# Gated recurrences in chunks of 64 in place of 128, with state products split by head over two PSUM banks

## The chip, the cores and the metric

The kernel runs on one core of one Trainium2 chip. The metric is the time of one execution on the device in microseconds (us). The kernel before took 2409.89 us, the median of three runs (2408.58 to 2411.97). All the traces named here are of single profiled executions on that core. PE is the matrix engine (PEld its weight loads), DVE the vector engine, ACT the scalar engine, POOL the general engine, SP the engine that issues most transfers. PSUM is the memory that PE writes its results to; it has eight banks, and a bank holds 128 partitions x 512 fp32 values.

## The reference, cut to what matters

One layer of a decoder trunk on 2048 tokens of width 1024. A token mixer holds three kinds of heads side by side: four retention heads, eight HGRN2 heads and four GLA heads. The last two are gated linear recurrences with a decay per key channel, which the change is mostly about. A convolution-gated MLP follows.

```python
def gated_state_chunkwise(q, k, v, log_f):
    # S_t = diag(exp(log_f_t)) S_{t-1} + k_t^T v_t,  o_t = q_t S_t, in chunks of 64
    def step(s, inp):
        qn, kn, vn, gn = inp
        cum = jnp.cumsum(gn, axis=2)
        rel = jnp.where(causal, cum[:, :, :, None, :] - cum[:, :, None, :, :], -jnp.inf)
        attn = jnp.einsum('bhid,bhjd,bhijd->bhij', qn, kn, jnp.exp(rel))
        o = jnp.einsum('bhij,bhje->bhie', attn, vn) + jnp.einsum('bhid,bhde->bhie', qn * jnp.exp(cum), s)
        last = cum[:, :, -1:, :]
        s_new = jnp.exp(last[:, :, 0, :])[..., None] * s + jnp.einsum('bhjd,bhje->bhde', kn * jnp.exp(last - cum), vn)
        return s_new, o
```

Every head has 64 value columns and a key width of 64 (32 for GLA). The result does not depend on the chunk length that a kernel picks.

## The kernel before, in words

**Blocks and units.** The 2048 tokens are cut into four blocks of 512 (`NB`, `TB`), and each block into four pieces of 128 (`NCH`). Heads come in units that fill the 128 partitions: four `h` units of two HGRN2 heads each, one `g` unit of four GLA heads (two halves, called subs), and two `r` units of two retention heads. In a block they run in the order h0, g, h1, h2, h3, r0, r1. Tiles carry the unit's name: `uh2_1` is the tile u of unit h1 in block 2. Every fp32 product here is made either from three fp32r products (`split3`, lines 292 to 294: the large projections, called gemms below) or as a plain fp32 product, which shows as two records in the trace.

**A gated unit** (`gated`, L713). The scores inside a piece of 128 tokens are built level by level: at level s (1, 2, 4 ... 64) the second half of every stretch of 2s tokens attends to the first half (`level`, L753), after q and k have been multiplied by the decays of that level (`faded`, L730, on DVE). `laid` (L771) puts the level's scores into the tile `at`. The levels are issued two at a time; level 64 stands alone. Then k is transposed (`kT`, L834), the state products are made (`u`, L843: per piece, keys of 128 tokens against values of 128 tokens), `carry` (L679) runs the recurrence over the four pieces on DVE, one `scalar_tensor_tensor` of 128x64 per piece, and copies the states into a block-diagonal tile W with ACT. `attn_out` (L664) makes the output of each piece: q against W (K = 128 rows, N = 128 columns) and per head the scores against the values (K = 128, N = 64), both as four products of 32 output rows that lie in four column groups of PE's array (`tiled`, L148). ACT copies the output out of PSUM, `post` normalises it, and 21 us later by the planner's clock `transposed` (L652) turns it round for the output projection.

**PSUM.** Four banks belong to the gemms (`acc_ps`), two to the levels (`lev_ps`) and two to everything that comes late in a unit (`late_ps`, L155): the diagonal products `dt` of the first level, kT, u, the output o, the transposed output oT, and the sums of squares `ss` and broadcasts `bc` of a norm (`rstd`, L363). A tile of `late_ps` can only be written when the readers of the tile that had its bank are done.

**What sets the order.** The program is written out once, and a small planner with its own clock (`Clock`) decides where between the gemms the steps of a unit are put: each step advances the clock by a constant (`adv(MO)` and the like) and asks to be called again after a gap (`yield`). Steps with a pair of times (`RIDE`) may ride along at a `clock.pick()` of another unit, or go alone at the later time. PE, DVE and ACT each work strictly through their own list; so a PE instruction that waits holds up all gemms behind it.

Of the kernel before, what the change touches and what calls it, by code (L numbers as in the profile page):

```python
# [49 lines left out]
M512, M256, MF, ML, MT, MO, MS = 0.227, 0.12, 0.224, 0.5, 0.44, 1.7, 0.85  # L50
# [74 lines left out]
def trunk(ctx, tc, xT, vecs, cvec, cst, rope, msk, wada, win, walow, wgla, wout, wup, wdown, out):  # L125
# [486 lines left out]
    wide = [p1.tile([P, NCH, P], F32, tag=f"W{i}", name=f"W{i}") for i in range(3)]  # L612
    for st in wide:
        G.memset(st[:], 0.0)
# [49 lines left out]
    def attn_out(name, b, attn, v, qn, W):  # L664


        ps = late_ps("o" + name)
        for c in range(NCH):
            oc = ps[:, c * P:(c + 1) * P]
            inter = not (b == 0 and c == 0)  # L670
            if inter:
                tiled(oc, qn[:, c * P:(c + 1) * P], W[:, c, :], stop=False)
            for hh in range(2):
                at, col = attn[hh]
                tiled(oc[:, hh * 64:hh * 64 + 64], at[:, (c * 2 + col) * P:(c * 2 + col + 1) * P],
                      v[:, c, hh * 64:hh * 64 + 64], start=not inter, stop=hh == 1 or not inter)
        return ps

    def carry(b, Sst, ps, decay):  # L679

        W = wide.pop(0)
        wide.append(W)
        at = pu.tile([P, NCH - 1, 64], F32, tag="Sc", name="Sc", bufs=2)
        halves = slice(0, 64), slice(64, P)
        if b:
            for rs in halves:
                S.copy(W[rs, 0, rs], Sst[rs, :])
        for c in range(NCH):
            last = c == NCH - 1
            dst, u = Sst[:] if last else at[:, c, :], ps[:, c * 64:c * 64 + 64]  # L690
            if b == 0 and c == 0:
                V.tensor_copy(dst, u)
            elif not last or b < NB - 1:
                V.scalar_tensor_tensor(dst, at[:, c - 1, :] if c else Sst[:], decay(c), u, op0=ALU.mult, op1=ALU.add)
        for rs in halves:
            S.copy(W[rs, 1:NCH, rs], at[rs, :, :])
        return W

    LEVELS = [1, 2, 4, 8, 16, 32, 64]
    EOFF = {2: 0, 4: 256, 8: 384, 16: 448, 32: 480, 64: 496, 128: 504}  # L700
# [12 lines left out]
    def gated(name, b, ui, pos, kq, q, decay, subs, qk, sel):  # L713
# [16 lines left out]
        def faded(li):  # L730

            s, ev = LEVELS[li], tree[li]
            nn = TB // (2 * s)
            qv = q[:].rearrange("p h (n t s) -> p h n t s", t=2, s=s)[:, :, :, 1, :]
            kv = kq[:].rearrange("p (n t s) -> p n t s", t=2, s=s)[:, :, 0, :]

            def of_q():
                return V.tensor_tensor(qv, qv, ev[:, :, 0:1].unsqueeze(1).to_broadcast([P, 2, nn, s]), op=ALU.mult)

            def of_k():  # L740
                return V.tensor_tensor(kv, kv, ev[:, :, 1:2].to_broadcast([P, nn, s]), op=ALU.mult)
            for op in (of_q, of_k) if li < 6 else (of_k, of_q):
                done_ = op()
            marked(done_)
# [8 lines left out]
        def level(li, first):  # L753

            s = LEVELS[li]
            w = max(32, 2 * s)
            o = 0 if first else 128
            for c in range(NCH):
                for k0 in [g for g in range(0, P, 32) if g % w < max(s, 32)]:
                    r0 = k0 // w * w  # L760
                    at = c * P + r0
                    n, p0 = (c, k0) if s <= 16 else (c // 2, k0 + s * (c % 2))
                    for ps, rs in zip(pss, parts):
                        if first:
                            rhs = qc[rs, :, at // 2:(at + w) // 2].rearrange("p h (n s) -> p h n s", s=s)
                        else:
                            rhs = q[rs, :, at:at + w].rearrange("p h (n t s) -> p h n t s", t=2, s=s)[:, :, :, 1, :]
                        T.matmul(ps[p0:p0 + 32, o + n * w:o + (n + 1) * w].rearrange("p (h n s) -> p h n s", h=2, s=s),
                                 (kc_ if first else kq)[rs, c * P + k0:c * P + k0 + 32], rhs, start=True, stop=True)

        def laid(li, first):  # L771
# [3 lines left out]
            o = 0 if first else 128  # L775
            cols = slice(o, o + (128 if s < 64 else 256))
# [21 lines left out]
        for li in range(0, 8, 2):  # L798
            pss = [lev_ps(f"lv{name}_{li}") for _ in parts]
            pair_ = li < 6  # L800
# [4 lines left out]
            if pair_:  # L805
                level(li, True)
                level(li + 1, False)
            else:
                level(li, False)
            with tc.high_priority(offset=CHAIN):  # L810
                faded(li + 1 if pair_ else li)
                if li < 4:
                    ahead(li + 2)
                if li == 0:
                    pairs = dots[:, 0:NCH * nh].rearrange("p (a n) -> p a n", n=len(subs))
                    for i, near in enumerate(nears):
                        V.copy_predicated(near[:], m_all[:, 80:112].unsqueeze(1).to_broadcast([P, 8, 32]),
                                          pairs[:, :, i:i + 1].to_broadcast([P, 8, 32]))
                laid(li, pair_)
                if pair_:  # L820
                    laid(li + 1, False)
                if li < 4:
                    faded(li + 2)
            adv((2 if pair_ else 1) * ML)
# [4 lines left out]
            if pair_:  # L829
                yield PAIR_GAP[two]  # L830
        yield 4.0
# [4 lines left out]
        with tc.high_priority(offset=CHAIN):  # L836
            S.copy(kT[:].rearrange("p c n -> p (c n)"), ps[:])
            if not two:
                r0, r1 = subs[0][0][1]
                S.copy(q[r0:r1, 0, :], q[r0:r1, 1, :])  # L840
# [11 lines left out]
        for i, (rows, v, sg) in enumerate(subs):  # L852
            if i:
                yield RIDE[1]
            o = pu.tile([P, NCH, P], F32, tag="o", name=f"o{name}_{i}")
            heads = [(at, i) for at in attns] if two else [(attns[0], hh) for hh in range(2)]
            ps = attn_out(f"{name}_{i}", b, heads, v, q[:, i, :], W)
            adv(MO)
            with tc.high_priority(offset=CHAIN):
                S.copy(o[:].rearrange("p c e -> p (c e)"), ps[:])  # L860
# [127 lines left out]
    def retention(nm, b, r, pos, a, kk, kc, q, vsg):  # L988
# [16 lines left out]
        with tc.high_priority(offset=CHAIN):  # L1005
            W = carry(b, Sst, ps, lambda c: gc)
# [17 lines left out]
        ps = attn_out(nm, b, [(at, hh) for hh in range(2)], v, qn, W)  # L1024
        o = pu.tile([P, NCH, P], F32, tag="o", name="o" + nm)
        qd = c_all[:, C_QD + 2 * r:C_QD + 2 * r + 2]
        with tc.high_priority(offset=CHAIN):
            V.tensor_tensor(o[:].rearrange("p c (h e) -> p c h e", e=64),
                            ps[:].rearrange("p (c h e) -> p c h e", h=2, e=64),
                            qd.unsqueeze(1).unsqueeze(3).to_broadcast([P, NCH, 2, 64]), op=ALU.mult)  # L1030
# [786 lines left out]
```

## Time and profile before

| | us |
|---|---|
| median of three runs | 2409.89 |
| profiled execution, first to last instruction | 2407.7 |
| PE busy | 2364.9 (98%) |
| DVE busy | 1818.2 (76%) |
| ACT busy | 1292.1 (54%) |
| level products of the h units made from q itself (N = 32, 64 and 128: levels up to 16, level 32, level 64) | 15.7, 7.2, 10.3 |
| output products against W: h, g, r | 26.1, 12.5, 12.3 |
| output products against v: h, g, r | 27.4, 13.4, 13.8 |
| state products u: h, r, g | 10.5, 5.2, 2.6 |

The profiled execution lies 2.2 us below the median of the runs, so its parts can be read as parts of that median. The token mixer and what is interleaved with it take about the first 1100 us; the MLP follows. Busy time of a group is the union of its own records, so that groups that alternate, as the last but one and the last but two rows do, are counted twice for part of the time. A matmul record of some 200 to 400 ns overlaps its neighbours: how much a batch costs is read from the starts, not from the durations.

### The profile page before, as it was taken

The numbers are of one execution on the slowest core, as the hardware profiler recorded it, in microseconds if no ns is written. First come the engines' busy times: TensorE is split into PE (matmuls) and PEld (weight loads), VectorE is DVE, ScalarE is ACT, GpSimd is POOL, SyncE is SP. The second block draws the span as 40 slices with busy tenths as digits, with TensorE's granted clock in tenths as the row PEclk, the third lists the DMA queues.
The fourth block names the chain that finished last, engine by engine and source line by source line (L and its number), as shares of the span: only waits on it lengthen the run. The fifth ranks groups of instructions, "written<-read, shape, count | busy, mean of one in ns | idle before, by whom it ended". The sixth has DMA issues, their size and how long they took to land.

```text
span 2407.7 us, 51890 instructions
## 1 busy us (share of the span) xinstructions
PE 2364.9 (98%) x20523; PEld 1961.5 (81%) x20523; DVE 1818.2 (76%) x3391; ACT 1292.1 (54%) x2311; POOL 153.9 (6%) x275
## 2 busy tenths in 40 slices
PE   7999999999999999999999999999999999999998
PEld 5787878888788888887888888888878888888887
DVE  7687866868577746877988888866888787778566
ACT  4675456744665457644555454554555555455452
POOL 1000100000000100001000000000010100000000
PEclk9999999999999999999999999999999999999999
DMA  7655676797788867788554444687765444548663
GB/s 272 234 187 185 235 262 236 279 330 261 255 305 296 279 203 276 266 280 280 171 172 154 143 158 145 225 282 223 240 198 166 145 149 145 150 151 277 205 198 116
DMA packets 228884, 525.78 MB, mean 218 GB/s; under 512 B 25848, under 2 KB 28832, under 8 KB 228640
## 3 DMA queue, kind: packets, MB, share of 16 engines
q1 hardware_dynamic: 225440, 511.98, 63.7%
q0 software_dynamic: 3200, 10.49, 1.2%
q8 instruction: 161, 2.64, 0.4%
q14 instruction: 83, 0.68, 0.1%
HBM read 392.87 MB, written 129.50 MB: 217 GB/s over the span
## 4 chain that ended last, share of the span: by engine, by line
PE 82%; DVE 8%; DMA 5%; ACT 4%; issue 1%; SPq 0%; DVEq 0%; POOL 0%; ACTq 0%
PE X L292 6%; PE X L294 6%; PE X L293 6%; PE dX L292 4%; PE dX L293 4%; PE dX L294 4%; PE Z L293 3%; PE Z L294 3%; PE Z L292 3%; PE psqkvgr L292 3%; PE psqkvgr L294 2%; PE psqkvgr L293 2%; PE y L292 2%; PE y L293 2%; PE y L294 2%; PE dY L292 2%
## 5 line engine op out<-in xcount | busy, mean ns | idle before, releaser
L293 PE MATMUL X<-B,A 128*128 128x512 f32 x572 | 222.8, 389 | 0.3 <-DVE B L1187 0.3
L292 PE MATMUL X<-B,A 128*128 128x512 f32 x572 | 223.0, 390 | 0.0
L294 PE MATMUL X<-B,A 128*128 128x512 f32 x572 | 222.6, 389 | 0.0
L1187 DVE TENSOR_TENSOR dA<-rd,dA 128x512 fp32r<-128x512 f32 x154 | 106.2, 690 | 91.3 <-ACT dA L1186 91.0
L1186 ACT CAST dA<-rd 128x512 fp32r<-128x512 f32 x154 | 95.6, 622 | 145.7 <-PE dX L294 62.8
L292 PE MATMUL dX<-dB,dA 128*128 128x512 f32 x396 | 154.0, 389 | 0.0
L293 PE MATMUL dX<-dB,dA 128*128 128x512 f32 x396 | 154.0, 389 | 0.0
L294 PE MATMUL dX<-dB,dA 128*128 128x512 f32 x396 | 154.0, 389 | 0.0
L1187 DVE TENSOR_TENSOR A<-s,A 128x512 fp32r<-128x512 f32 x176 | 120.6, 686 | 37.8 <-ACT A L1186 37.7
L1186 ACT CAST A<-s 128x512 fp32r<-128x512 f32 x176 | 108.6, 617 | 60.7 <-PE Z L294 43.5
L292 PE MATMUL psvgh<-hvgh,ha 128*128 128x256 f32 x480 | 139.6, 291 | 0.0
L293 PE MATMUL psvgh<-lvgh,ha 128*128 128x256 f32 x480 | 135.7, 283 | 0.0
L294 PE MATMUL psvgh<-hvgh,ha 128*128 128x256 f32 x480 | 135.6, 283 | 0.0
L293 PEld LDWEIGHTS X<-B,A 128*128 128x128 f32 x572 | 107.4, 188 | 23.2 <-DVE B L1187 1.1
L292 PEld LDWEIGHTS X<-B,A 128*128 128x128 f32 x572 | 107.4, 188 | 22.9 <-ACT u L1493 0.7
L294 PEld LDWEIGHTS X<-B,A 128*128 128x128 f32 x572 | 107.4, 188 | 22.1
L293 PE MATMUL Z<-B,A 128*128 128x512 f32 x308 | 120.6, 392 | 2.3 <-DVE B L1187 2.1
L292 PE MATMUL Z<-B,A 128*128 128x512 f32 x308 | 120.3, 391 | 0.2
L294 PE MATMUL Z<-B,A 128*128 128x512 f32 x308 | 119.9, 389 | 0.0
L1186 ACT CAST A<-r 128x512 fp32r<-128x512 f32 x132 | 82.3, 624 | 63.8 <-PE Z L294 58.2
L1187 DVE TENSOR_TENSOR A<-r,A 128x512 fp32r<-128x512 f32 x132 | 90.6, 687 | 31.3 <-ACT A L1186 30.7
L1187 DVE TENSOR_TENSOR dB<-rb,dB 128x512 fp32r<-128x512 f32 x154 | 105.6, 687 | 7.5 <-ACT dB L1186 7.1
(491 smaller groups left out, 6786.4 us busy)
## 6 DMA issues: line engine op xcount, KB each, us to landing
gs<-yv SPq DMA_DIRECT2D x154, 256.0 KB, 3.0
rb<-gs SPq DMA_DIRECT2D x154, 256.0 KB, 4.3
r<-wup SPq DMA_DIRECT2D x143, 256.0 KB, 3.4
s<-sumsu SPq DMA_DIRECT2D x132, 256.0 KB, 3.2
wada<-wada SPq DMA_DIRECT2D x48, 512.0 KB, 4.5
rd<-sumsd SPq DMA_DIRECT2D x88, 256.0 KB, 4.2
rd<-wdown SPq DMA_DIRECT2D x66, 256.0 KB, 3.9
x<-xT SPq DMA_DIRECT2D x64, 256.0 KB, 5.3
```

The source lines that it names most:

```text
L292: T.matmul(ps, lhs[0], rhs[0], start=first, stop=False, skip_group_check=more)
L293: T.matmul(ps, lhs[0], rhs[1], start=False, stop=False, skip_group_check=more)
L294: T.matmul(ps, lhs[1], rhs[0], start=False, stop=last, skip_group_check=more)
L1186: S.copy(hi, src)
L1187: marked(V.tensor_tensor(lo, src, hi, op=ALU.subtract))
```

## The change

Gated units now work in chunks of 64: level 64 is gone, `carry` makes eight states a block, and u is made per chunk of 64 tokens, that is with 64 rows, the even chunks from partitions 0 to 63 into one late bank and the odd ones from partitions 64 to 127 into another. The products of q with the states are made per head, 64 rows and 64 columns each, head 0 into one late bank and head 1 into another, for gated and for retention units (these keep chunks of 128). The block-diagonal tiles W, their zeroing and the ACT copies into them are gone, as is a copy of half of q; the states are used from the tile Sc in which DVE leaves them. The output is copied out of PSUM by two ACT instructions of 128x256; for retention units these take the scaling that one DVE instruction did. The planner's cost of an output step, `MO`, goes from 1.7 to 1.3, and a `yield 4.0` and one `clock.pick()` vanish with level 64.

```diff
-M512, M256, MF, ML, MT, MO, MS = 0.227, 0.12, 0.224, 0.5, 0.44, 1.7, 0.85
+M512, M256, MF, ML, MT, MO, MS = 0.227, 0.12, 0.224, 0.5, 0.44, 1.3, 0.85
...
-    def attn_out(name, b, attn, v, qn, W):
-        ps = late_ps("o" + name)
+    def attn_out(name, b, attn, v, ql, Sc, chunk):
+        pss = [late_ps(f"o{name}_{hh}") for hh in range(2)]
         for c in range(NCH):
-            oc = ps[:, c * P:(c + 1) * P]
-            inter = not (b == 0 and c == 0)
-            if inter:
-                tiled(oc, qn[:, c * P:(c + 1) * P], W[:, c, :], stop=False)
-            for hh in range(2):
+            cs = slice(c * 64, c * 64 + 64)
+            carried = [g for g in range(0, P, 32) if b or chunk(c, g)]
+            for hh, ps in enumerate(pss):
+                for g in carried:
+                    T.matmul(ps[g:g + 32, cs], ql(hh)[:, c * P + g:c * P + g + 32],
+                             Sc[hh * 64:hh * 64 + 64, chunk(c, g), :], start=True, stop=False)
+            for hh, ps in enumerate(pss):
                 at, col = attn[hh]
-                tiled(oc[:, hh * 64:hh * 64 + 64], at[:, (c * 2 + col) * P:(c * 2 + col + 1) * P],
-                      v[:, c, hh * 64:hh * 64 + 64], start=not inter, stop=hh == 1 or not inter)
-        return ps
+                for g in range(0, P, 32):
+                    k0 = (c * 2 + col) * P + g
+                    T.matmul(ps[g:g + 32, cs], at[:, k0:k0 + 32], v[:, c, hh * 64:hh * 64 + 64],
+                             start=g not in carried, stop=True)
+        return pss
...
-    LEVELS = [1, 2, 4, 8, 16, 32, 64]
+    LEVELS = [1, 2, 4, 8, 16, 32]
...
-        ps = late_ps("u" + name)
+        pss = [late_ps(f"u{name}_{n}") for n in range(2)]
         for c in range(NCH):
-            tiled(ps[:, c * 64:c * 64 + 64], kT[:, c, :],
-                  lambda g: subs[g // 32 % len(subs)][1][:, c, g // 64 * 64:g // 64 * 64 + 64])
+            for n, ps in enumerate(pss):
+                rs = slice(64 * n, 64 * n + 64)
+                for g in range(0, P, 32):
+                    T.matmul(ps[g:g + 32, c * 64:c * 64 + 64], kT[rs, c, g:g + 32],
+                             subs[g // 32 % len(subs)][1][rs, c, g // 64 * 64:g // 64 * 64 + 64], start=True, stop=True)
         with tc.high_priority(offset=CHAIN):
-            W = carry(b, Sst, ps, lambda c: cur[:, c:c + 1])
+            Sc = carry(b, Sst, [pss[n % 2][:, n // 2 * 64:n // 2 * 64 + 64] for n in range(8)], lambda n: cur[:, n:n + 1])
...
             with tc.high_priority(offset=CHAIN):
-                S.copy(o[:].rearrange("p c e -> p (c e)"), ps[:])
+                for hh, ps in enumerate(pss):
+                    S.copy(o[:, :, hh * 64:hh * 64 + 64], ps[:, 0:256].rearrange("p (c e) -> p c e", e=64))
```

Three places show what the change does to the lists of the engines. In the rows, 32x64 is the shape of one product's output, "x4" four such products one after another.

PE, the output of unit h1 in block 2. Before, both kinds of products take 128 rows of the array (q against W1, then the scores ath against the values vh):

```order
L151 MATMUL oh2_1_0_10428<-W1_115,qbh2_1_9410 32x128 x4
L151 MATMUL oh2_1_0_10428<-vh2_1_9423,ath2_1_0_9475 32x64 x8
L151 MATMUL oh2_1_0_10428<-W1_115,qbh2_1_9410 32x128 x4
L151 MATMUL oh2_1_0_10428<-vh2_1_9423,ath2_1_0_9475 32x64 x8
L151 MATMUL oh2_1_0_10428<-W1_115,qbh2_1_9410 32x128 x4
```

Now the L670 rows take 64 rows of the array and the L676 rows 128:

```order
L670 MATMUL oh2_1_0_0_10662<-Sc_10490,qbh2_1_9634 32x64 x4
L670 MATMUL oh2_1_0_1_10663<-Sc_10490,qbh2_1_9634 32x64 x4
L676 MATMUL oh2_1_0_0_10662<-vh2_1_9646,ath2_1_0_9761 32x64 x4
L676 MATMUL oh2_1_0_1_10663<-vh2_1_9646,ath2_1_0_9761 32x64 x4
L670 MATMUL oh2_1_0_0_10662<-Sc_10490,qbh2_1_9634 32x64 x4
L670 MATMUL oh2_1_0_1_10663<-Sc_10490,qbh2_1_9634 32x64 x4
```

The 32-row products alternate between the two forms four times in an output, and the output fills two late banks where it filled one. Over the whole program PE's list goes between 64-row and 128-row products of 32 columns 246 times where it did so 7 times.

PE, where unit h2 of block 2 begins. Before, its diagonal products dth2_2 stood between the transposes and the state products of unit h1:

```order
L768 MATMUL lvh2_1_6_9993<-qbh2_1_9410,kh2_1_9171 32x128 x8
...
L834 MATMUL kTh2_1_10123<-c_all_86,kh2_1_9171 128x128 x4
...
L151 MATMUL dth2_2_10138<-c_all_86,qkh2_2_9910 32x2 x16
...
L768 MATMUL lvh2_2_2_10255<-qc_112,kc_113 32x32 x16
...
L151 MATMUL uh2_1_10296<-vh2_1_9423,kTh2_1_10128 32x64 x16
```

Now they stand right behind the state products, and wait for DVE:

```order
L819 MATMUL kTh2_1_10294<-c_all_86,kh2_1_9470 128x128 x4
...
L830 MATMUL uh2_1_0_10456<-vh2_1_9646,kTh2_1_10299 32x64 x4
L830 MATMUL uh2_1_1_10457<-vh2_1_9646,kTh2_1_10299 32x64 x4
...
L151 MATMUL dth2_2_10501<-c_all_86,qkh2_2_10220 32x2 [waits DVE_49,PE_49]
L151 MATMUL dth2_2_10501<-c_all_86,qkh2_2_10220 32x2 x15
```

The level-64 products (lvh2_1_6) are gone. What dth2_2 waits for is the seventh of the eight DVE steps of `carry` that read uh2_1_0, whose bank it takes.

DVE, the carry of unit h3 in block 2. Before, four steps, each but the last with one other instruction behind it:

```order
L694 SCALAR_TENSOR_TENSOR Sc_11243<-S3_108,eh2_3_10212,uh2_3_11226 128x64 [waits PE_49]
L983 TENSOR_TENSOR kkr2_0_10758<-ra1r2_0_11151,c_all_86 128x512 [waits DVE_49]
L694 SCALAR_TENSOR_TENSOR Sc_11243<-Sc_11243,eh2_3_10212,uh2_3_11226 128x64 [waits DVE_49]
L1068 TENSOR_TENSOR wsu15_0_11203<-wsu15_0_11203,wsu15_1_11204 128x512
...
L694 SCALAR_TENSOR_TENSOR S3_108<-Sc_11243,eh2_3_10212,uh2_3_11226 128x64 [waits DVE_49]
```

Now eight, with seven others between them:

```order
L691 SCALAR_TENSOR_TENSOR Sc_11601<-S3_108,eh2_3_10569,uh2_3_0_11567 128x64 [waits PE_49]
L965 TENSOR_TENSOR rb1r2_0_11509<-ra1r2_0_11507,roper2_0_11134 128x8x32
L691 SCALAR_TENSOR_TENSOR Sc_11601<-Sc_11601,eh2_3_10569,uh2_3_1_11568 128x64 [waits DVE_49,PE_49]
L966 TENSOR_TENSOR ra1r2_0_11507<-ra1r2_0_11507,roper2_0_11134 128x512 [waits DVE_49]
...
L1052 TENSOR_TENSOR wsu15_2_11561<-wsu15_1_11560 128x512 [waits DMAHW7_49,DMAHW4_49]
L691 SCALAR_TENSOR_TENSOR Sc_11601<-Sc_11601,eh2_3_10569,uh2_3_0_11567 128x64 [waits DVE_49]
L1053 TENSOR_TENSOR wsu15_2_11561<-wsu15_2_11561,wsu15_0_11559 128x512 [waits DMAHW6_49,DVE_49]
L691 SCALAR_TENSOR_TENSOR S3_108<-Sc_11601,eh2_3_10569,uh2_3_1_11568 128x64 [waits DVE_49]
```

On PE the transposes oTh2_2 now come three gemm products behind uh2_3 (twelve before), and wait for the seventh of these steps.

More of the change, by code (lines that the diff above doesn't have):

```diff
@@ L692, in carry @@
+        return pss
+    def carry(b, Sst, us, decay):
+        Sc = pu.tile([P, 8, 64], F32, tag="Sc", name="Sc", bufs=2)
+        if b:
+            S.copy(Sc[:, 0, :], Sst[:])
+        for n, u in enumerate(us):
+            last = n == len(us) - 1
+            dst = Sst[:] if last else Sc[:, n + 1, :]
+            if b == 0 and n == 0:
                 V.tensor_copy(dst, u)
             elif not last or b < NB - 1:
-                V.scalar_tensor_tensor(dst, at[:, c - 1, :] if c else Sst[:], decay(c), u, op0=ALU.mult, op1=ALU.add)
@@ L828, in gated @@
                 yield None
[L829 to L831 removed]
+            yield PAIR_GAP[two]
         ps = late_ps("kT" + name)
```

72 lines of the change are left out of this document (24 added, 48 removed).

## The prediction

> **What bounds the kernel now.** First the page: its span, PE's busy time, PE's row and the clock's row of the 40 slices, and the chain of waits by engine.
>
> ```profile
> span 2407.7 us, 51890 instructions
> PE 2364.9 (98%) x20523; PEld 1961.5 (81%) x20523; DVE 1818.2 (76%) x3391; ACT 1292.1 (54%) x2311; POOL 153.9 (6%) x275
> PE   7999999999999999999999999999999999999998
> PEclk9999999999999999999999999999999999999999
> PE 82%; DVE 8%; DMA 5%; ACT 4%; issue 1%; SPq 0%; DVEq 0%; POOL 0%; ACTq 0%
> ```
>
> PE is never at rest after the first slices, and the chain that ended last runs on it for 82% of the span. What the change does to PE's list, and every wait that it puts there, therefore shows in the time; DVE (76% busy) and ACT (54%) matter by when they let PE go on. The busy times by stretch (columns: span, then PE, PEld, DVE, ACT, POOL busy, clock, DMA) say how little PE waits in the mixer:
>
> ```profile
> 100.00:600.00 500.00, 489.19 (x6937) 411.96 (x6936) 382.90 (x938) 289.37 (x592) 26.18 (x46) 1.00 0.70 243
> 600.00:1100.00 500.00, 495.36 (x6942) 413.51 (x6941) 345.00 (x883) 289.68 (x601) 25.25 (x45) 1.00 0.78 273
> ```
>
> Idle are 10.8 + 4.6 = 15.4 us. The MLP after 1100 us is not touched.
>
> **Level 64 goes.** PE's timeline where it stood alone (start, length, then what):
>
> ```profile
> 218.87 0.40 PE L294 MATMUL psqkvgr<-hqkvgr,ha 128*128 128x512 f32 x1
> 219.19 0.64 PE L768 MATMUL lvh<-qbh,kh 128*32 128x128 f32 x16
> 219.77 0.50 PE L292 MATMUL psqkvgr<-hqkvgr,ha 128*128 128x512 f32 x1
> 220.10 0.40 PE L293 MATMUL psqkvgr<-lqkvgr,ha 128*128 128x512 f32 x1
> 220.34 0.39 PE L294 MATMUL psqkvgr<-hqkvgr,ha 128*128 128x512 f32 x1
> ```
>
> From 218.87 to 220.10 are 1.23 us, where two gemm steps take 0.46: the batch costs 0.77. Of 20 units 16 have it alone; 4 share the entry with another batch and save the products' own 0.46 only. 16 x 0.77 + 4 x 0.46 = 14.2 us gained. The removed batches would take 16 entries from gemm to 32-column products out of PE's list, and it has only 11 fewer (127 before, 116 now), so 5 x (0.77 - 0.46) = 1.5 us come back.
>
> **The outputs pay for changing the array's form.** The end of an output, and the retention scores (64 rows) behind it:
>
> ```profile
> 1056.05 0.43 PE L151 MATMUL oh<-W,qbh 128*32 128x128 f32 x8
> ...
> 1056.95 0.40 PE L151 MATMUL oh<-W,qbh 128*32 128x128 f32 x8
> 1057.17 0.41 PE L151 MATMUL oh<-vh,ath 128*32 128x64 f32 x16
> 1057.40 0.40 PE L151 MATMUL oh<-W,qbh 128*32 128x128 f32 x8
> 1057.61 0.41 PE L151 MATMUL oh<-vh,ath 128*32 128x64 f32 x16
> 1057.95 1.16 PE L1015 MATMUL scr<-qr,kcr 64*32 64x128 f32 x64
> ```
>
> A piece takes 0.45 us, 0.22 for W and 0.23 for the scores. Between batches of one form the next begins 0.18 before the last has ended (1057.17 + 0.41 against 1057.40); at the step from 128*32 to 64*32 it is 0.07 (1057.61 + 0.41 against 1057.95), so 0.11 is lost, and the first batch of a form is 0.03 longer (0.43 against 0.40). The way back, from 64 to 128 rows, is there too:
>
> ```profile
> 114.16 0.51 PE L768 MATMUL lvg<-qbg,kg 64*32 64x64 f32 x30
> 114.60 0.43 PE L151 MATMUL oh<-vh,ath 128*32 128x64 f32 x16
> ...
> 372.92 0.72 PE L768 MATMUL lvg<-qc,kc 64*32 64x32 f32 x62
> ```
>
> Again 0.07 of overlap and 0.43 for the first. I take 0.14 a change. The 64-row records come one per 8.7 ns (0.72 less one record's 0.19, over 61) to 10 ns (0.51 less 0.23, over 29), so the 16 new products against the states take 0.15 where W took 0.22. An output: 4 x (0.15 - 0.22) + 7 changes x 0.14 = +0.70; 32 outputs, +22.4 us. Bounds: 0.11 a change gives +0.49 (15.7), and 0.17 gives +0.91 (29). The Trainium skill's page TensorEngine Tiling (Array Packing) says under Key Properties that a change of the tiling mode, not of the tile alone, drains the engine. By that rule the edit loses, and these rows agree. Under Theoretical Speedup the same page has up to 2x for a small dimension of at most 64. By that alone the outputs would get cheaper, as in the third rival below, which gives 2388.
>
> **State products.** 32 records become 64 of 64 rows:
>
> ```profile
> 776.59 0.65 PE L151 MATMUL uh<-vh,kTh 128*32 128x64 f32 x32
> ...
> 780.03 0.60 PE L656 MATMUL oTh<-c_all,oh 128*128 128x128 f32 x4
> ```
>
> 0.65 less one record's 0.22 is 0.43; 64 x 9 ns are 0.58: +0.15 x 20 units = +3.0 us. PE's own work thus grows by 22.4 + 3.0 + 1.5 - 14.2 = +12.7 us (bounds +4 and +19).
>
> **The larger part: PE waits for late banks.** The state products now hold both late banks, and the next user of a bank waits on PE, with all gemms queued behind it, until the seventh of the eight carry steps has read it. DVE's timeline for the unit just shown:
>
> ```profile
> 780.47 0.28 DVE L694 SCALAR_TENSOR_TENSOR Sc<-S,eh,uh 128x64 f32<-128x64 f32 x1
> 780.66 0.69 DVE L983 TENSOR_TENSOR kkr<-ra1r,c_all 128x512 f32<-128x512 f32 x1
> 781.26 0.28 DVE L694 SCALAR_TENSOR_TENSOR Sc<-Sc,eh,uh 128x64 f32<-128x64 f32 x1
> 781.45 0.69 DVE L1068 TENSOR_TENSOR wsu<-wsu,wsu 128x512 f32<-128x512 f32 x1
> 782.06 0.28 DVE L694 SCALAR_TENSOR_TENSOR Sc<-Sc,eh,uh 128x64 f32<-128x64 f32 x1
> ```
>
> With another instruction between them the steps come 0.80 apart; the first began 3.2 us after the products' end (777.24). The transposes at 780.03 took the other bank, before the steps were done: that way out is gone. With next to nothing between, steps come 0.31 apart:
>
> ```profile
> 747.96 0.27 DVE L694 SCALAR_TENSOR_TENSOR Sc<-Sc,eh,uh 128x64 f32<-128x64 f32 x1
> 748.15 0.16 DVE L182 TENSOR_SCALAR rsn<-msn 128x4 int32<-128x4 int32 x1
> 748.27 0.28 DVE L694 SCALAR_TENSOR_TENSOR Sc<-Sc,eh,uh 128x64 f32<-128x64 f32 x1
> ```
>
> Other instructions in the way, and what frees the banks of dots and outputs:
>
> ```profile
> L738 DVE TENSOR_TENSOR qbh<-qbh,eh 128x512 f32<-128x512 f32 x96 | 66.5, 692 | 5.1 <-ACT qc L749 2.6 <-PE lvh L768 2.1
> L741 DVE TENSOR_TENSOR kh<-kh,eh 128x256 f32<-128x256 f32 x96 | 40.3, 420 | 4.7 <-PE lvh L768 4.7
> L817 DVE COPY_PREDICATED nearh<-m_all,dth x16: 439/445/461, 72.5 to 1012.3; 128x256 f32<-128x256 uint32 x16
> L860 ACT COPY oh<-oh 128x512 f32<-128x512 f32 x16 | 9.3, 583 | 4.8 <-PE oh L151 4.6
> ```
>
> The waits, by the new lists:
>
> - Transposes three gemm products (0.7 us, and 0.1 for the entry) behind u of h3, four times. Three have an instruction between every two steps: 6 x 0.80 + 0.28 = 5.1; block 0 has four such: 4 x 0.80 + 2 x 0.31 + 0.28 = 4.1. Less 0.8, with the first step 1 us late (0 at the best, 3.2 in the rows above): 3 x 5.3 + 4.3 = 20.2.
> - Transposes behind u of h2, blocks 1 to 3. One step, three others (0.4, 0.69, 0.42), six steps: 3.6; the first held back some 0.9 by the level work in front of it; less 0.8: 3.7 x 3 = 11.1.
> - Diagonal products of h2 directly behind u of h1, blocks 1 to 3: 0.28 + 0.69 + 6 x 0.31, with 0.1 to start: 2.9 x 3 = 8.7.
> - Four more users 1.4 to 2 us behind u: about 1 each, 4.
> - 17 places where a bank's user comes within 2 us of the last one, waiting for one copy of a dot (0.45), an output (0.58 at most) or a transpose: 0.65 each, 11.
>
> Sum 55.0; with no step late and 0.2 at the small places 38; with the first step 3.2 late at h3, and DVE and ACT as far behind elsewhere, 87. Other engines catch up while PE waits, so I let a third of the 15.4 us of present idle time go: -4 (bounds 0 and -15). On DVE itself the lost decays of level 64 (0.692 + 0.420) and the four added steps (4 x 0.28) cancel; ACT only loses work. Both stay off the path except in these waits.
>
> **The sum.** 2407.7 + 12.7 + 55.0 - 4 = 2471.4 in the span of the profiled execution; the runs' median lies 2.2 above it: **2474 us**. The bounds add up to 2407.7 + 4 + 38 - 15 + 2.2 = 2437 and 2407.7 + 19 + 87 + 2.2 = 2516.
>
> **Rivals.** *The clock falls* (2495): waits of 4 to 5 us are as long as this one at the start:
>
> ```profile
> 8.60:13.20 4.60, 0.01 (x1) 0.00 (x0) 3.37 (x5) 4.29 (x8) 0.00 (x0) 0.90 1.02 388
> 13.20:19.00 5.80, 5.65 (x18) 4.10 (x19) 4.70 (x17) 2.72 (x4) 0.00 (x0) 0.50 1.03 416
> ```
>
> After 4.6 us of rest the granted clock was 0.50 for 5.8 us, half of which is lost, 2.9; at the seven longest waits that is 20 us. Against it: the other long waits lie below 4. The Trainium skill (TensorE: Matmul & The Clock Gate, Part 1: The HAM clock gate) puts the fall after an idle window of about 3.4 us; these two rows agree.
>
> *The banks are free in time* (2423): if DVE runs ahead and the small places cost nothing, only PE's 12.7 us stay. For it: DVE has a quarter of its time free. Against: a chain of dependent steps cannot be shorter than 7 x 0.31 = 2.2.
>
> *Row packing pays and nothing waits* (2388): 64-row products side by side without loss at a change save 32 x 4 x 0.07 = 9 in the outputs beside the 14.2, less 3.0 and 1.5, and some idle goes: -21. It decides only if a change costs under 0.04 us. The rows say 0.11.
>
> *The parts cancel* (2410): changes at 0.11, half the gain of level 64 more from shared entries, waits within the present idle.
>
> **Chances.** Forecast 0.64, clock 0.14, free banks 0.12, cancel 0.04, packing 0.06. The two below and half of the free-bank case lie outside the range at the low end, some of the clock's case at the high end: 2428 to 2506; the forecast's own range is 2437 to 2498. What the measurement can tell from no change is 0.2% (4.8 us): faster 0.06, within 0.04, slower 0.90.
>
> **What would show it.** In the waits of PE, rows of oTh and dth released by the carry, some 40 us together; PE idle in 100 to 1100 of 50 to 80 us; outputs about 0.7 us longer between the first and last start; clock row still 9. Wrong is it if PE's idle time stays near 15 us, or an output is no longer than before.

## The result and the profile after

The changed kernel took 2517.05 us, the median of four runs (2512.88 to 2520.79), against 2409.69 us for the kernel before on the same chip: a ratio of 1.0441, 95% interval 1.0426 to 1.0456. It is slower, as forecast, but by 107 us where 64 were forecast, and outside the range. The profiled execution took 2515.09 us and its span is 2513.0 us, 105.3 more than the span before.

The page after, in the rows that were read before: span, busy times, PE's and the clock's row of the 40 slices, and the chain of waits by engine.

```profile
span 2513.0 us, 54320 instructions
PE 2413.6 (96%) x21787; PEld 1983.0 (79%) x21787; DVE 1816.9 (72%) x3403; ACT 1252.3 (50%) x2210; POOL 153.0 (6%) x272
PE   7998999889998999989999999999999999999998
PEclk9999999999998999999999999999999999999999
PE 80%; DVE 9%; DMA 5%; ACT 4%; issue 2%; SPq 0%; DVEq 0%; POOL 0%; ACTq 0%
```

PE is busy 48.7 us longer and idle 56.6 longer. The clock's row shows one 8 among the nines, and it would be easy to pass over. The busy times by stretch (span, PE, PEld, DVE, ACT, POOL, then the clock) say more:

```profile
100.00:600.00 500.00, 462.43 (x6926) 379.84 (x6925) 346.73 (x867) 248.53 (x506) 22.21 (x41) 0.96 0.63 219
600.00:1100.00 500.00, 473.15 (x6824) 389.46 (x6823) 319.05 (x808) 255.91 (x499) 23.68 (x40) 0.97 0.70 243
```

In the 1000 us where PE rested 15.4 us before it now rests 64.4, and the mean clock is 0.96 and 0.97 where it was 1.00. What PE waits for (total, times, longest):

```profile
PE oTh L653 <- DVE Sc L691: 25.9, 7, 5.3
PE dth L151 <- DVE Sc L691: 13.8, 4, 5.3
...
PE ssn L151 <- DVE Sc L691: 4.2, 2, 3.6
```

These 43.9 us are waits for the carry to leave a late bank. The kernel before has one such wait, of 2.0 us:

```profile
PE ssn L151 <- DVE S L694: 2.0, 1, 2.0
```

One of the new ones on PE's timeline, block 0 (start, length, then what):

```profile
240.43 0.86 PE L830 MATMUL uh<-vh,kTh 64*32 64x64 f32 x64
...
241.80 0.40 PE L294 MATMUL psqkvgr<-hqkvgr,ha 128*128 128x512 f32 x1
246.38 1.09 PE L653 MATMUL oTh<-c_all,oh 128*128 128x128 f32 x4 [4.19 <-DVE Sc L691]
...
249.40 0.63 PE L294 MATMUL psqkvgr<-hqkvgr,ha 128*128 128x512 f32 x1
249.83 0.63 PE L292 MATMUL psqkvgr<-hqkvgr,ha 128*128 128x512 f32 x1
...
251.58 0.39 PE L294 MATMUL psqkvgr<-hqkvgr,ha 128*128 128x512 f32 x1
251.81 0.40 PE L292 MATMUL psqkvgr<-hqkvgr,ha 128*128 128x512 f32 x1
```

The wait is 4.19 us. What the forecast had left to a rival stands behind it: gemm products that begin 0.23 us apart at 251.6 begin 0.43 apart at 249.4. The same place in stretches of 3.4 us:

```profile
240.90:244.30 3.40, 1.29 (x35) 0.71 (x29) 3.40 (x10) 0.00 (x0) 0.00 (x0) 1.00 0.19 76
244.30:247.70 3.40, 1.32 (x6) 1.25 (x7) 2.15 (x7) 0.19 (x1) 0.00 (x0) 0.50 0.69 233
247.70:251.10 3.40, 3.40 (x9) 2.64 (x8) 0.75 (x1) 0.50 (x1) 0.00 (x0) 0.50 0.00 0
251.10:254.50 3.40, 3.40 (x16) 2.81 (x15) 1.22 (x1) 1.05 (x1) 0.00 (x0) 1.00 0.02 5
```

The granted clock is 0.50 for 6.8 us, and runs on at half speed after PE is busy again. Between 100 and 1150 us the trace has 18 such periods, 6 of 6.8 us and 12 of 3.4: 82 us. The kernel before has none between 43 us and its end.

So the 105 us have three parts. I take each PE record from its start to the next start (or its own end), price those that lie in a half-clock period at the mean of their kind at full clock, and call what is left of them "clock". Against the kernel before, in us:

| profiled run | ratio of the runs (95%) | span | PE's own work | PE idle | clock |
|---|---|---|---|---|---|
| changed kernel | 1.0441 (1.0426, 1.0456) | +105.3 | +13.2 | +56.6 | +35.5 |
| e1_evac | 1.0192 (1.0177, 1.0207) | +50.5 | +14.1 | +17.4 | +18.9 |
| e2_grouped | 1.0366 (1.0345, 1.0386) | +92.9 | -6.0 | +64.9 | +34.0 |
| e3_both | 1.0125 (1.0099, 1.0151) | +27.5 | -4.2 | +23.1 | +8.7 |
| e6_busy | 1.0462 (1.0445, 1.0480) | +111.2 | +76.2 | +24.7 | +10.3 |
| e6b_busy6 | 1.0371 (1.0346, 1.0397) | +91.0 | +47.9 | +33.0 | +10.0 |
| e7_outputs | 1.0141 (1.0120, 1.0161) | +43.4 | +21.1 | +15.5 | +6.8 |
| e10_dots | 1.0116 (1.0100, 1.0131) | +28.9 | -1.2 | +22.6 | +7.5 |
| e11_dots_kt | 1.0129 (1.0114, 1.0144) | +34.5 | -3.7 | +25.7 | +12.3 |
| e12_onebank | 1.0076 (1.0061, 1.0091) | +18.5 | -6.7 | +15.6 | +9.6 |
| e13_rest1 | 1.0149 (1.0132, 1.0166) | +38.9 | +6.5 | +24.7 | +7.6 |
| e14_rest2 | 1.0302 (1.0284, 1.0320) | +70.9 | -1.1 | +45.1 | +26.7 |
| e15_mo | 1.0398 (1.0370, 1.0426) | +101.7 | +12.1 | +51.3 | +38.1 |

The division between own work and clock is good to some 8 us: e13_rest1 and e14_rest2 carry the same added products and differ by 7.6 us in own work. With medians in place of means the parts of the changed kernel come out the same, and when kinds are drawn otherwise its clock's part lies between 30 and 36 us and its own work between 13 and 19. Each ratio is to runs of the kernel before beside it.

### The profile page after: what moved, and what is told of

It reads as the page before. It is cut to its first block, busy times and chain, and to the rows that moved or that the text cites. A ratio compares the mean times of both kernels' runs of the same rounds, so it can differ in the third digit from the quotient of the medians.

```text
span 2513.0 us, 54320 instructions
## 1 busy us (share of the span) xinstructions
PE 2413.6 (96%) x21787; PEld 1983.0 (79%) x21787; DVE 1816.9 (72%) x3403; ACT 1252.3 (50%) x2210; POOL 153.0 (6%) x272
## 4 chain that ended last, share of the span: by engine, by line
PE 80%; DVE 9%; DMA 5%; ACT 4%; issue 2%; SPq 0%; DVEq 0%; POOL 0%; ACTq 0%
PE X L292 6%; PE X L294 6%; PE X L293 6%; PE dX L293 4%; PE dX L294 4%; PE dX L292 4%; PE Z L293 3%; PE Z L294 3%; PE Z L292 3%; PE psqkvgr L292 2%; PE psqkvgr L293 2%; PE psqkvgr L294 2%; PE y L292 2%; PE y L294 2%; PE y L293 2%
## 5 line engine op out<-in xcount | busy, mean ns | idle before, releaser
L1175 DVE TENSOR_TENSOR A<-s,A 128x512 fp32r<-128x512 f32 x176 | 120.5, 686 | 38.4 <-ACT A L1174 38.2
L293 PEld LDWEIGHTS X<-B,A 128*128 128x128 f32 x572 | 107.3, 188 | 23.1 <-DVE B L1175 0.9
```

The costliest lines, as they stand in the source:

```text
L293: T.matmul(ps, lhs[0], rhs[1], start=False, stop=False, skip_group_check=more)
L1175: marked(V.tensor_tensor(lo, src, hi, op=ALU.subtract))
```

## The experiments

**Free the banks at once** (e1_evac)**.** In the changed kernel, two ACT copies take the state products out and the carry reads the copy:

```diff
+        us = pu.tile([P, 2, 256], F32, tag="us", name="us" + name, bufs=1)
         with tc.high_priority(offset=CHAIN):
-            Sc = carry(b, Sst, [pss[n % 2][:, n // 2 * 64:n // 2 * 64 + 64] for n in range(8)], lambda n: cur[:, n:n + 1])
+            for n, ps in enumerate(pss):
+                S.copy(us[:, n, :], ps[:, 0:256])
+            Sc = carry(b, Sst, [us[:, n % 2, n // 2 * 64:n // 2 * 64 + 64] for n in range(8)], lambda n: cur[:, n:n + 1])
```

> The changed kernel, with one thing added in the gated units: two ACT copies take both banks of the state products (128x256 each) into SBUF at once, and the carry steps read them there, so the banks are free after the copies and not after the seventh carry step. PE's list is the same. Theory W (waits for the two banks, and the halved clock that follows each such wait, are most of the 105 us): PE waits behind the carry, 43.9 us now in the rows of oTh, dth and ssn, fall below 10; PE idle from 100 to 1150 us goes from 72 to about 35; the half-clock periods from 18 to about 7 (those of other causes); time about 2455 us, 2440 to 2470. Theory P (PE's own longer work, outputs above all, is most of it, and the waits only move): 2495 to 2515. Theory D (DVE is late whatever it reads; the outputs would then wait for the states in place of the banks): the idle time stays above 60 us in other rows, over 2490.

2458.8 us (2455.4 to 2460.2), ratio 1.0192. In the traces PE's list is the same but for four places, where the records of two small batches stand in another order. In its waits the carry is gone, and the copies stand in its place:

```profile
PE oh L670 <- DVE msn L373: 4.0, 2, 3.1
...
PE dth L151 <- ACT ush L835: 3.4, 3, 1.8
...
PE oTh L653 <- ACT ush L835: 2.1, 3, 0.7
```

The group of the copies (after the bar: busy time and mean ns of one):

```profile
L835 ACT COPY ush<-uh 128x256 f32<-128x256 f32 x32 | 10.4, 381 | 5.2 <-PE uh L830 4.7
```

43.9 us of waits became 5.5, idle time from 100 to 1150 us went from 72 to 32, and the clock's part from 35.5 to 18.9. Half-clock periods fell from 18 to 10, three more than expected. Theory W holds; P and D fall.

**One change of form in an output** (e2_grouped)**.** The same products, those against the states first:

```diff
+        def put(hh, g, c, lhs, rhs, stop):
+            T.matmul(pss[hh][g:g + 32, c * 64:c * 64 + 64], lhs, rhs, start=(hh, g) not in begun, stop=stop,
+                     skip_group_check=True)
+            begun.add((hh, g))
         for c in range(NCH):
...
+            for hh in range(2):
+                for g in [g for g in range(0, P, 32) if b or chunk(c, g)]:
+                    put(hh, g, c, ql(hh)[:, c * P + g:c * P + g + 32], Sc[hh * 64:hh * 64 + 64, chunk(c, g), :], False)
+        for c in range(NCH):
...
+                    put(hh, g, c, at[:, k0:k0 + 32], v[:, c, hh * 64:hh * 64 + 64], c == NCH - 1)
```

> The changed kernel, with the same products of each output in another order: first all products against the states (64 rows) of the four pieces, then all score products (128 rows), so one change of the array's form in the output and not seven. Nothing else moves on PE. Theory F (a change of form costs 0.10 to 0.14 us each, which is why an output takes 2.53 us and 1.90 before): an output takes 1.75 to 1.95 us, and the time falls by 32 x 6 x 0.13 = 25 us to about 2492, 2487 to 2500. Theory R (the longer output is the two heads' separate products, twice as many 64-row records, and changes of form are nearly free): an output stays within 0.2 us of 2.53 and the time within 2512 to 2521.

2500.99 us (2494.7 to 2503.8), ratio 1.0366. PE's timeline of one output, first of the changed kernel (its first and last batches and the gemm behind it), then of this one:

```profile
1081.24 0.34 PE L670 MATMUL oh<-Sc,qbh 64*32 64x64 f32 x16
1081.51 0.43 PE L676 MATMUL oh<-vh,ath 128*32 128x64 f32 x16
...
1083.41 0.43 PE L676 MATMUL oh<-vh,ath 128*32 128x64 f32 x16
1083.77 0.50 PE L292 MATMUL pshqh<-ha,hhqh 128*128 128x512 f32 x1
```

```profile
1072.14 0.86 PE L668 MATMUL oh<-Sc,qbh 64*32 64x64 f32 x64
1072.93 1.10 PE L668 MATMUL oh<-vh,ath 128*32 128x64 f32 x64
1073.96 0.50 PE L292 MATMUL pshqh<-ha,hhqh 128*128 128x512 f32 x1
```

From start to the next gemm 2.53 us against 1.82: 0.71 for six changes, 0.12 each. That is theory F, though the time stands 1 us above its range: it fell by 0.75% (18 us) and not by 32 x 0.71 = 23, for PE's own work fell 19 us and its idle time grew 8. PE came sooner to the same late banks.

**Both** (e3_both)**.**

> Both edits together: state products copied out at once, and one change of form in each output. If the two act on different things the gains add: 2517 less about 62 (the copies) less about 25 (the order) is 2430, 2412 to 2446. If the shorter outputs only bring PE sooner to the same late banks, the second gain is lost: 2450 or more. Below the kernel before (2409.7) only if the other small waits go as well.

2440.43 us (2437.0 to 2450.7), ratio 1.0125. The two gains add, within the range given: with the banks free, the shorter outputs keep their worth.

**Useless work in place of rest** (e6_busy, e6b_busy6)**.** Behind u at the ten places of the carry's longest waits:

```diff
+        if ui == 3 or b and ui in (1, 2):
+            keep_going(lev_ps("idle" + name), 13)
```

> The changed kernel, with useless work added: 13 matmuls (128x256, some 2.7 us together at 0.21 each) into a level bank behind the state products of the units h3 of every block and h1 and h2 of blocks 1 to 3, the ten places where PE then waits 2.8 to 5.3 us for the carry. The rest of every list is the same. PE works there instead of resting, and waits as much less. Theory C (the rest halves the clock for 3.4 to 6.8 us after each of these waits, and that is a cost of its own beside the rest): PE idle from 100 to 1150 falls from 72 to about 46, the half-clock periods behind these ten places, 51 us now, mostly go, and the time falls by 15 to 25 us, to 2492 to 2502, though 27 us of work were added. Theory N (the clock's fall costs little, because what follows a wait is not bound by it): 2515 to 2525, and up to 2544 if the waits do not shrink.

2522.8 us, ratio 1.0462, which is what theory N had said. But the thirteen products took 5.5 to 5.8 us a place and not 2.7, for each is two records; I had read the row of the startup's twenty records as twenty products. 58 us had been added, more than the waits could hold, so the time tells nothing by itself. In the trace idle fell by 32 us and the clock's part by 25, about what was added. I ran it again with six:

> As e6_busy, with 6 useless matmuls at each of the ten places in place of 13. In e6_busy the 13 took 5.5 to 5.8 us and not 2.7 (two records each), 58 us together, longer than the waits that they were to fill (38 us). Six take 12 of its records, 2.6 us a place, 26 us together, and fit into all ten waits. Theory C (the halved clock behind each wait is a cost of its own): idle from 100 to 1150 us falls from 72 to about 46, the added work cancels that, the half-clock periods fall from 82 us to about 35, and the time falls by 15 to 23 us, to 2494 to 2502, though nothing useful is done sooner. Theory N (the clock costs little): 2513 to 2521, since work and saved waits cancel.

2504.14 us (2495.5 to 2507.9), ratio 1.0371 (1.0346 to 1.0397) against 1.0441 (1.0426 to 1.0456) without the useless work. The added work takes 30.0 us in its own row (26 had been reckoned) and 34.7 in the table's column of own work, and the kernel became 0.7% (17 us) faster. The group of the added work, then the waits of this run:

```profile
L424 PE MATMUL idleh<-c_all 128*128 128x256 f32 x120 | 30.0, 401 | 0.0
```

```profile
PE oTh L653 <- DVE Sc L691: 6.7, 5, 2.2
PE ssn L151 <- DVE Sc L691: 5.2, 2, 3.3
...
PE dth L151 <- DVE Sc L691: 4.7, 3, 2.5
```

The waits for the carry are 16.6 us instead of 43.9, and all idle time is 23.6 us less: the work saved less rest than it took itself. What was gained is the clock: 10.0 us instead of 35.5. Theory C holds, though the time is 2 us above its range; theory N falls.

**What a rest costs** (e13_rest1, e14_rest2)**.** The kernel before, with a rest of a chosen length at 16 places: a small product, POOL fills its operand k times, a small product again.

```diff
+        if not two:
+            bank = lev_ps("rest" + name)
+            T.matmul(bank[0:32, 0:8], rest[:, 0:32], rest[:, 0:8], start=True, stop=True)
+            with tc.high_priority(offset=CHAIN):
+                for _ in range(k):
+                    G.memset(rest[:], 0.0)
+            T.matmul(bank[0:32, 8:16], rest[:, 0:32], rest[:, 0:8], start=True, stop=True)
```

> The kernel before, with a short rest of PE added at 16 places and nothing else: behind the state products of each gated unit h, PE does one small product, waits until POOL has filled its 64-column operand 4 times, and does another small one. From rows of POOL (0.10 for 2 columns, 0.31 for 256, and 0.05 between dependent fills) four fills are some 0.8 us, with the way there and back 1.1 us of rest. Theory C (the clock halves for the next 3.4 us only where PE rested about 1.6 us or more within one of the clock's own 3.4 us windows, as the half-clock periods of the changed kernel stand against its rests): no new half-clock period (2 at most), cost 16 x 1.1 and some 2 us for the products: 0.5% to 1.0% slower than before. If every rest costs its length alone whatever it is, the same.

> The same with 12 fills at each of the 16 places, some 2.7 us of rest. Theory C: 12 to 15 new half-clock periods of 3.4 us (6.8 at some), each costing some 1.5 us more than the rest itself; 16 x 2.7 + 2 + about 14 x 1.5 = 66 us, 2.3% to 3.2% slower than before, so three to four times the cost of the shorter rests for 2.5 times their length. Theory N (a rest costs its length and no more): 45 us, 1.6% to 2.0%, or less if other engines catch up meanwhile.

PE's waits, k = 4 and then k = 12:

```profile
PE resth L855 <- POOL rest L854: 15.8, 16, 1.0
```

```profile
PE resth L855 <- POOL rest L854: 42.5, 16, 2.7
```

Of the 16 rests of 1.0 us three were followed by a half-clock period, each with 1.2 us or more of other rest just before it; of the 16 rests of 2.7 us thirteen were. One of each, by stretches of 3.41 us:

```profile
795.28:798.69 3.41, 2.41 (x43) 1.77 (x43) 1.75 (x5) 0.00 (x0) 0.60 (x4) 1.00 0.98 376
798.69:802.10 3.41, 3.41 (x18) 2.83 (x17) 3.11 (x8) 1.83 (x4) 0.00 (x0) 1.00 0.79 320
```

```profile
780.60:784.01 3.41, 0.74 (x60) 0.65 (x51) 2.11 (x7) 0.87 (x3) 1.81 (x12) 1.00 0.50 191
784.01:787.42 3.41, 3.41 (x94) 2.49 (x85) 2.12 (x11) 0.00 (x0) 0.00 (x0) 0.50 0.02 5
```

The longer rests cost 3.02%, as theory C had it. The shorter ones cost 1.49%, more than the 0.5 to 1.0% expected: besides the three periods behind them, the program has two behind rests that I had not put there, one of them a stall of 4.3 us for which the profile names no releaser. So the step between the two is 35 us for 26.7 us of rest, and not the three- to fourfold cost that I expected. Both programs hold such a stall, of 4.3 and of 4.9 us.

**The outputs alone** (e7_outputs)**.** The kernel before with the change's `attn_out` and copies, the tiles W gone with it; chunks of 128, level 64 and one bank of state products stay.

> The kernel before, with the change's outputs alone: per head on 64 rows into two banks, copies per bank, the retention's output on ACT. Chunks stay 128, level 64 stays, the state products stay in one bank with four carry steps. Theory W (the outputs cost their own length and little more; the waits come from the state products' two banks): 32 outputs x 0.63 us (2.53 against 1.90 in the two traces) are +20, some small waits for the second bank and their clock +8: 2438 us, 2428 to 2450, with PE idle from 100 to 1100 us of 20 to 30. Rival (the outputs' two banks are what starves the late banks): idle above 40 us, half-clock periods at ten places or more, 2465 to 2490.

2449.19 us (2443.2 to 2452.9), ratio 1.0141, at the upper end of theory W's range. The outputs make 34 us, about a third of the whole loss. In the profiled run, which is 43.4 us longer than that of the kernel before, 21.1 are length, about what 32 x 0.63 gives, 15.5 idle time and 6.8 the clock. The other two thirds are left to chunks of 64, and to what both do to each other. Idle from 100 to 1150 us was 29 us, so the rival falls. Part of that idle I had not expected; PE's timeline inside one output:

```profile
206.08 0.42 PE L676 MATMUL oh<-vh,ath 128*32 128x64 f32 x12
208.41 0.30 PE L676 MATMUL oh<-vh,ath 128*32 128x64 f32 x4 [1.92 <-issue]
```

It stops for 1.92 us between products of one batch. More on this below.

**What is left over** (e10_dots, e11_dots_kt, e12_onebank)**.** To e3_both I added, one after the other: the diagonal products in unused columns of a level bank (`dots = pss[0][:, 256:256 + NCH * nh]`); the transposes of the keys in a level bank (`ps = lev_ps("kT" + name)`); and, without this last one, the outputs of the h units in one bank, the state products over 128 rows of the zero-padded queries.

> As e3_both, and the diagonal products of each gated unit go into unused columns of the first level bank in place of a late bank, so 20 users of the late banks are gone. Theory L (what is left over the kernel before, 28 us in e3_both's 2440, is other users of the two late banks waiting for each other: idle 38.7 us against 17.4 and the clock behind it): PE waits of dth (4.1 us) vanish, other late users find a bank free more often, idle falls to about 30 and the half-clock periods by a third: 2430 us, 2420 to 2437. If the waits only move to other users: 2437 to 2443.

> As e10_dots, and the transposes of the keys go into a level bank too (the one that the pair of levels 4 and 8 has left), so 40 of the late banks' users are gone. Theory L: the wait of outputs for the copy of kT (2.6 us in e3_both) goes too, idle about 26: 2425 us, 2413 to 2435. If the level banks are then the scarce ones (level pairs wait for the copy of kT): 2435 or more.

> As e10_dots, and the 16 units h make their outputs in one late bank: the state products take all 128 rows of the units' zero-padded queries, per head, 64 columns, as the score products do, so there is no change of form in them, and one copy as before. The other 16 outputs stay grouped in two banks. Theory L (what is left over the kernel before are the two banks of the outputs): PE waits at oh and oTg fall, idle from 36.9 to about 28, 2425 us, 2415 to 2436. Theory I (what is left are the stalls inside batches of many small products, in which the profile names no releaser, 13 us in e10_dots against 3 before, and late DVE work): no gain, 2436 to 2446, with these stalls still above 10 us.

Ratios 1.0116, 1.0129 and 1.0076. The first two are no better than e3_both's 1.0125: theory L fell there, the idle time only moved (23.1, 22.6 and 25.7 us over the kernel before). The third gained 0.4% on e10_dots, within theory L's range; its largest row of waits is now one without a releaser:

```profile
PE oh L688 <- issue: 9.4, 5, 3.4
```

So theory L has the time right, and theory I that such stops remain. At 2429.07 us it is the best version with chunks of 64 that I have, and still 0.76% slower than the kernel before. No version here beats that one.

**The planner's price** (e15_mo)**.**

```diff
-M512, M256, MF, ML, MT, MO, MS = 0.227, 0.12, 0.224, 0.5, 0.44, 1.3, 0.85
+M512, M256, MF, ML, MT, MO, MS = 0.227, 0.12, 0.224, 0.5, 0.44, 1.7, 0.85
```

> The changed kernel with one edit taken back: the planner again prices an output at 1.7 us and not at 1.3 (an output really takes 2.53 us in the changed kernel). That alone shifts a few dozen places of PE's list by some products, the units' own order stays. Theory W (the two banks of the state products and the clock, wherever the planner puts the next user by a product or two): still slower than before by 3.6% to 4.8%, PE waits behind the carry of 35 to 50 us, 14 half-clock periods or more. Rival O (the new order that the smaller price makes puts the users of the banks too near): under 3%, waits behind the carry under 25 us.

2507.62 us (2501.7 to 2514.9), ratio 1.0398 (1.0370 to 1.0426). Its waits for the carry are 47.6 us, and the two largest rows are the same:

```profile
PE oTh L653 <- DVE Sc L691: 33.2, 7, 6.5
PE dth L151 <- DVE Sc L691: 13.1, 4, 5.4
```

The order that the smaller price makes is worth about 0.4% of the 4.4%, and is not the cause.

## Why the prediction was wrong, point by point

**Level 64 and the entries** (-14.2 and +1.5, together -12.7). In the records the levels fell by 10.7 us and the gemms around them by 4.6: -15.3. The first number holds however the kinds are drawn; the second is less than the 8 us to which the division is good. Right.

**The outputs** (+0.70 each, 22.4 in all). 2.53 against 1.90 us is +0.63; all output records together +23.0. A change of form was taken at 0.14, and e2_grouped measured 0.12 with nothing else changed. Right, and the rival that needed a change under 0.04 is out.

**The state products** (+0.15 each, 3.0 in all). A batch is 0.86 us long where it was 0.65, +0.21, and all of them make +5.5. I had taken 9 ns a record from other 64-row products; here it is (0.86 - 0.22) / 63, 10 ns. Too small, by 2.5 us. PE's own work came to +13.2 against 12.7. That it is so close is in part luck: 2.6 us more were gained at the levels and 2.5 more lost here, and the division does not reach to half a microsecond.

**The waits** (55.0, less 4 of present idle: 51). Measured: idle +56.6. By class: transposes behind u of h3, forecast 20.2, measured 4.19 + 4.15 + 5.27 + 3.35 = 17.0; behind u of h2 11.1 and 9.0; diagonal products behind u of h1 8.7 and 5.32 + 3.61 + 3.30 = 12.2, since there too the carry's first step came late. These ten make 40.0 forecast and 38.2 measured; the misses of the three classes (3.2, 2.1 and -3.5) nearly cancel. The rows of oTh and dth have 39.7 us where the forecast's sign was some 40. One more, 3.6 us at a norm's sums at 363 us, I had not seen. All waits behind the carry, with the four users just behind u, are 44.0 forecast and 43.9 measured, the 3.6 among them. Other idle time grew by 14.7 us (56.6 less 43.9, and the 2.0 of before), where 11 less 4 had been forecast; 5 of the 14.7 are stops without a releaser, which the forecast did not know. The mechanism of the waits was right. The first step late by about a microsecond is what the trace shows; at the transposes quoted above the products end at 241.29, and DVE, in the middle of other work, goes from there to the step that frees the bank:

```profile
241.62 1.22 DVE L350 TENSOR_TENSOR lqkvgr<-rqkvgr,hqkvgr 128x1024 fp32r<-128x1024 f32 x1
242.75 0.22 DVE L689 COPY Sc<-uh 128x64 f32<-128x64 f32 x1
...
245.33 0.91 DVE L691 SCALAR_TENSOR_TENSOR Sc<-Sc,eh,uh 128x64 f32<-128x64 f32 x3
```

**The clock: the step that failed.** The sum had no term for it. It was a rival with a chance of 0.14 and a price of 20 us, and it is 35.5 us. The forecast's own terms, 2407.7 + 13.2 + 56.6, give 2477.5 in the span, 6 us from what they were forecast to give; the clock is the rest. Two readings failed in it. First, I took one row, 4.6 us of rest at the start, for the length that a rest must have, and argued that "the other long waits lie below 4". The 0.90 in that row already says that the clock had fallen 0.9 us before the rest was over. In the changed kernel, a window with 1.6 us of rest is enough (third to last column: the clock); below it stands one with 1.5 that was not:

```profile
302.28:305.69 3.41, 1.84 (x96) 1.22 (x91) 2.62 (x5) 1.64 (x4) 1.55 (x2) 1.00 0.75 247
305.69:309.10 3.41, 3.19 (x10) 2.71 (x11) 2.49 (x7) 1.85 (x4) 0.00 (x0) 0.51 0.17 65
203.30:206.71 3.41, 1.89 (x59) 1.44 (x61) 3.15 (x10) 1.59 (x3) 0.00 (x0) 1.00 0.28 104
206.71:210.12 3.41, 3.41 (x79) 2.86 (x69) 3.38 (x9) 1.15 (x2) 0.00 (x0) 1.00 0.40 153
```

Second, the trace of the kernel before held the row against me, and I did not look for it. 36 us after the start PE rested 0.89 and 0.62 us in one window, and the next 3.41 us ran at half clock:

```profile
36.20:39.61 3.41, 1.91 (x10) 1.26 (x9) 3.41 (x6) 0.72 (x1) 1.05 (x2) 1.00 0.83 228
39.61:43.02 3.41, 3.41 (x15) 3.12 (x14) 3.41 (x7) 0.72 (x1) 1.89 (x2) 0.50 0.55 168
```

By this row each of the ten carry waits (2.8 to 5.3 us) was likely to cost one or two periods of 3.4 us at half speed, about 1.7 us each where PE works all through them; a rest that two windows share can escape, as 3 of the 16 rests of 2.7 us did. All ten did cost it. Ten waits, five of them with double periods, are 51 us at half clock; the rest of the 82 came from eight rests of 1.5 to 3.6 us that are not among the ten. The rule from the Trainium skill that I put beside the rival (TensorE: Matmul & The Clock Gate, Part 1: The HAM clock gate: a fall after an idle window of about 3.4 us) says it too weakly: by these rows half of such a window is enough. The same section says that the window runs freely and does not start with the kernel, and there the trace agrees: all periods of one run begin on one grid of 3.413 us.

**The other rivals.** *Banks free in time* did not happen; e1_evac shows what it would have been worth, 2.5%. *The parts cancel* did not happen either. That the clock's row would "still be 9" was wrong in one digit only, though a third of the loss was in it: a row of tenths over slices of 63 us hides 82 us at half clock that are spread over 18 places.

## What to carry to other kernels

A rest of PE in a stream that is bound by PE has two prices: its length, and, where a window of 3.4 us holds more than 1.8 us of it (from 1.4 us on in some cases), about another 1.7 us for each window at half clock behind it. So look for the granted clock in stretches of 3.4 us behind each wait that is there already, and price every wait that a change adds with both. When a product is spread over two banks of a pool of two, name the next user of the pool and the last reader of the banks before anything else; two copies out of the banks on an engine with time (0.38 us each here) were worth 2.5%; even work of no use in the gaps was worth 0.7%.

## What the chip showed that was not expected

**The clock's windows.** Over the fourteen traces of this study I cut the time from 25 us to 2390 into each run's own grid of 3.413 us and took windows at full clock. All 95 with more than 1.82 us of rest were followed by half clock; of 82 with 1.4 to 1.82 us 34 were, of 135 with 0.86 to 1.4 six, and of 9201 with less none. A window at half clock with more than 0.7 us of rest was followed by another in 28 of 28 cases, one with less in 8 of 144. Why windows between 0.86 and 1.82 differ stays open; many of the falls in that band lie among batches of small products: 30 of the 40 windows hold more than 40 records of PE, against 88 of the 177 that were not followed by half clock.

**Stops inside batches.** PE stops for 1 to 5 us between products of one batch, and the profile names no releaser ("issue"). All of PE's idle time without a releaser is 3.1 us in the kernel before, 8.2 in the changed one and 18.0 in e12_onebank. Of 109 rests over 0.9 us inside batches in these traces 55 ended 2.15 to 2.65 us after a 16 KB transfer of the queue that the profile calls instruction had begun, where chance would give about 6. Split by releaser it is sharper: 52 of the 54 without one did, and 3 of the 55 with one. The kernel before has 161 such transfers for 41,046 records of PE and its weight loads, the changed one 170 for 43,574: some 256 records for each in both. That PE there waits for its next instructions is likely from this; it was not tested. It would make many small products cost more than their records. The stops change place from one edit to the next: e13_rest1 and e14_rest2 have one of 4.3 and 4.9 us that the kernel before does not have.
